# A decoder block in fp32 on one core: the first block's values summed quarter by quarter, and one written order for the first half

## The chip, the core and the metric

One core of one Trainium2 chip runs the whole program in one launch. The metric is device time in microseconds, the median of several runs of the same kernel. Beside these runs there is one profiled execution, taken by the hardware profiler; its rows are what is read below.

Six names recur. PE is the matrix engine (TensorE), PEld its weight loads, DVE is VectorE, ACT is ScalarE, POOL is GpSimd, and SP (SyncE) is the queue from which most transfers are issued. Memory on the core is SBUF; matrix products land in PSUM, which has eight banks of 128 x 512 fp32 numbers.

## The reference

A hybrid decoder block on a sequence of 2048 positions, D_MODEL 1024, eight heads of 128. Cut to what the kernel must compute:

```
c_act = silu(c)
mod = c_act @ w_mod + b_mod                    # 1024 -> 3 x 1024
shift, scale, gate = split(mod, 3)
h = rms_norm(x, g_norm) * (1 + scale) + shift  # 2048 x 1024
proj = h @ w_in                                # 2048 x 8192
x_rnn, z_rnn, q, k, v, z_attn, g_r, g_a = split(proj, 8)
xc = causal_depthwise_conv(x_rnn, conv_w, conv_b)
hr = rg_lru(xc, w_a, b_a, w_x, b_x, lam, positions)
y_rnn = (hr * silu(z_rnn)) @ w_out_rnn
o = dilated_attention_mixture(rope(q), rope(k), v)   # windows (128,1), (512,4), (2048,16)
y_attn = (o * silu(z_attn)) @ w_out_attn
merged = sigmoid(g_r + bg_r) * y_rnn + sigmoid(g_a + bg_a) * y_attn
x = x + gate * (merged @ w_o)
return rms_norm(x, g_final)
```

Nothing of `h @ w_in` can begin before a part of `mod` is known: `shift` and `scale` of the channels that the product sums over. That is why the start of the kernel consists of the modulation product.

## The kernel before

**Precision.** Every fp32 product is made of three faster products (fp32r): the high part of one operand by the high part of the other, high by low, and low by high. `mm3` issues the three through `mm` (line 151). The high part of an operand is written by ScalarE (`hi_act`, line 159), the low part, which is the operand minus its high part, by GpSimd (`lo_pool`, line 165) or VectorE (`lo_dve`, line 168). So nearly all of TensorE's instructions stand at line 151, and nearly all splits at three lines; rows are told apart by their tiles. `S` is a ring of seven tiles that hold split operands, `R` a ring of five raw tiles behind them, `T` the activations, `hf` a scratch copy. X, Z, W, V and Y are PSUM tags of pool `pj` (X has two banks, the others one), and `pg` has two banks.

**Staging.** The sequence is cut into four blocks of 512 rows, whose positions are stored so that `r` = 0..3 runs over row groups. Two halves (f = 0, 1) take two blocks each, one "even" (operands named B11 and B21, one for each half of the 1024 channels, `KH` = 4 slices `k` of 128 in each) and one "odd". For each half:

1. *Values.* `values_half` computes the v columns as plain products. Four groups `m` of 256 columns (two heads), two blocks, two halves `g` of a block's rows: 48 products of 128x128 by 128x256 for each (m, block, g), 768 in a half. `values_by_halves` does m = 0 for the even block, `values` the rest. `store_values` evicts a PSUM bank to an `ev` tile on ScalarE (line 725) and stores it to DRAM (`vN`, line 727).
2. *Strassen pairs.* The other column groups are done by pairs of 2 x 2 blocks with seven products of 12 matmuls each instead of eight. Their activation operands are B11, B21 and the combinations T1..T4 that `build_odd` makes from the odd block. Weights are loaded, split and combined ahead of their product: `operand_events` gives each step a due time in products, four products early, and `pump` runs what is due. The first half stores its split weights to DRAM, and the second reloads them.

Then attention, the output products and the final norm.

**Activations.** `load_x` loads a block; `norm_x` squares the rows on ScalarE (line 509), makes the reciprocal root, and scales each of the four row groups on VectorE (line 511). `turned` transposes four 128 x 128 tiles of slice k into one PSUM bank (line 521). `build` writes slice k: `h = scale * t + shift`, the high part on ScalarE (line 531), a full copy on ScalarE (line 534) where it must be kept, or on VectorE, and the low part on VectorE. `build_odd` does the eight slices of the odd block, and then, in eight steps, the differences (`tt`, on VectorE) and the splits of T1..T4.

**The start.** In this order in the text: load of the even block (2 x 1 MB on SP), 30 idle matmuls on constant data, parameter rows loaded and transposed (line 606), `ca = silu(c)` (lines 610 and 611), `norm_x`, four quarters of w_mod's shift and scale columns (`load_mod`, 2 x 1 MB each). Then for each quarter j: of the eight k, VectorE sums KV = 4 in rows (`acc`, lines 646 and 648), TensorE takes the other four and the `acc` rows as products with one output row (`W<-T,ca` and `W<-acc,ones`, line 151), ScalarE copies the row out (`mrow`, line 654), TensorE turns it into columns (`pg<-ones,mrow`), VectorE adds the bias and makes `mod` and `gs` (lines 666 and 667), idle matmuls follow, and the two slices k of this quarter are built. No value product of m = 0 is issued until two whole quarters (`kh` = 0) of it are built, and `w` of the values comes in halves of four k (`load_wv_half`).

**Order.** All of this is laid out by a scheduler that simulates a timeline (`schedule_with_timeline_sim`), within some orders imposed by `tc.issue_after(...)`. In stretches under `tc.manual_schedule()` the instructions go to the engines exactly as the program writes them. Before, such a stretch ran from the first half's first Strassen pair to the half's end, and another over the attention; the first half's values and the whole second half were left to the scheduler.

## Time and profile before

| | |
|---|---|
| median of three runs | 2324.31 us (2319.95, 2324.31, 2330.45) |
| profiled execution, span | 2322.0 us, 34101 instructions |
| PE busy | 2233.7 us (96%) |
| PEld busy | 1868.9 us (80%) |
| DVE busy | 1347.5 us (58%) |
| ACT busy | 1238.5 us (53%) |
| POOL busy | 971.1 us (42%) |
| transfers | 573.41 MB, 247 GB/s on the mean |
| mean granted TensorE clock | 0.984 |

The stages of the profiled execution, by TensorE's rows: the start to 49.35 us, the first half's values to 150.5, its Strassen pairs to about 750, the second half's values to 849, its Strassen pairs to 1476, attention and its products to about 2060, output to the end.

How to read the rows. A timeline row is: start, busy time, engine, line, operation, output tile <- input tiles, shape, and how many of them in a row; in brackets, how long the engine stood idle before it and what ended that. A window row gives the busy time of each engine in a stretch with the number of instructions, then the granted TensorE clock (1.00 is full), the share of the transfer engines and the rate. A group row of the page is: busy time of the group, mean ns of one | idle time of the engine just before them. A row of the waits is: engine, what waited <- what it waited for: us in all, times, mean us.

### The profile page before, as it was taken

The numbers are of one execution on the slowest core, as the hardware profiler recorded it, in microseconds if no ns is written. First come the engines' busy times: TensorE is split into PE (matmuls) and PEld (weight loads), VectorE is DVE, ScalarE is ACT, GpSimd is POOL, SyncE is SP. The second block draws the span as 40 slices with busy tenths as digits, with TensorE's granted clock in tenths as the row PEclk, the third lists the DMA queues.
The fourth block names the chain that finished last, engine by engine and source line by source line (L and its number), as shares of the span: only waits on it lengthen the run. The fifth ranks groups of instructions, "written<-read, shape, count | busy, mean of one in ns | idle before, by whom it ended". The sixth has DMA issues, their size and how long they took to land.

```text
span 2322.0 us, 34101 instructions
## 1 busy us (share of the span) xinstructions
PE 2233.7 (96%) x11459; PEld 1868.9 (80%) x11461; DVE 1347.5 (58%) x2424; ACT 1238.5 (53%) x2412; POOL 971.1 (42%) x734
## 2 busy tenths in 40 slices
PE   8999999999979998999999999999989898989998
PEld 4998788888858997877888877888879797868887
DVE  4828787768483706344444362367666777667343
ACT  4737667668433625555546311567768777534211
POOL 1457576766465333323111020446565655433100
PEclk9999999999989999999999999999999999999999
DMA  7367787887989487998776897979988888798532
GB/s 262 105 216 246 248 290 252 291 282 256 295 253 299 125 266 269 318 312 283 247 227 201 280 290 234 294 245 270 274 252 253 240 249 243 232 313 276 170 123 95
DMA packets 429013, 573.41 MB, mean 247 GB/s; under 512 B 72135, under 2 KB 293027, under 8 KB 427813
## 3 DMA queue, kind: packets, MB, share of 16 engines
q1 hardware_dynamic: 390996, 451.47, 63.3%
q10 hardware_dynamic: 37648, 119.70, 13.3%
q8 instruction: 91, 1.49, 0.3%
q14 instruction: 86, 0.70, 0.1%
q0 software_dynamic: 192, 0.05, 0.0%
HBM read 357.18 MB, written 213.91 MB: 246 GB/s over the span
## 4 chain that ended last, share of the span: by engine, by line
PE 50%; DMA 9%; DVE 4%; ACT 3%; issue 2%; POOL 1%; SPq 1%; ACTq 0%; DVEq 0%; POOLq 0%
PE pj L151 11%; PE pq L151 8%; PE X L151 7%; PE V L151 7%; PE o L151 3%; PE Y L151 3%; PE sc L151 3%; PE Z L151 3%; PE W L151 3%; DMA R<-yaT 1%; DMA vraw<-vN 1%; DMA R<-oT 1%; PE pT L1419 1%; PE pg L151 1%; DMA wD<-s 1%
## 5 line engine op out<-in xcount | busy, mean ns | idle before, releaser
L151 PE MATMUL pj<-yh,S 128*128 128x512 f32 x1024 | 369.1, 405 | 5.5 <-DMA S<-wD 4.2
L151 PE MATMUL V<-T,S 128*128 128x512 f32 x1344 | 338.7, 401 | 22.6 <-DVE t L451 9.6
L151 PE MATMUL X<-T,S 128*128 128x512 f32 x1344 | 332.5, 396 | 3.9 <-ACT u L384 3.9
L165 POOL TENSOR_TENSOR S<-R,S 128x512 fp32r<-128x512 f32 x168 | 251.9, 1510 | 181.2 <-ACT S L159 66.0
L151 PEld LDWEIGHTS V<-T,S 128*128 128x128 f32 x1344 | 257.6, 193 | 86.5 <-ACT S L159 7.9
L151 PEld LDWEIGHTS X<-T,S 128*128 128x128 f32 x1344 | 253.8, 189 | 64.4 <-ACT u L384 4.4
L151 PEld LDWEIGHTS pj<-yh,S 128*128 128x128 f32 x1024 | 194.2, 190 | 42.8 <-DVE fg L1626 4.6
L151 PE MATMUL pj<-yl,S 128*128 128x512 f32 x512 | 202.0, 395 | 0.0
L1335 ACT ACTIVATE pp<-pp,st 128x256 f32<-128x256 f32 (+3 forms) x256 | 134.0, 524 | 107.1 <-DVE st L1334 106.3
L165 POOL TENSOR_TENSOR S<-s,S 128x512 fp32r<-128x512 f32 x84 | 129.0, 1536 | 136.4 <-ACT S L159 94.6
L151 PE MATMUL W<-T,S 128*128 128x512 f32 x672 | 167.2, 397 | 0.4 <-POOL S L165 0.4
L151 PE MATMUL Z<-T,S 128*128 128x512 f32 x672 | 165.7, 395 | 0.0
L151 PE MATMUL Y<-T,S 128*128 128x512 f32 x672 | 165.4, 395 | 0.0
L151 PEld LDWEIGHTS W<-T,S 128*128 128x128 f32 x672 | 126.9, 190 | 30.8 <-issue 0.9
L151 PEld LDWEIGHTS Y<-T,S 128*128 128x128 f32 x672 | 126.7, 189 | 29.5
L151 PEld LDWEIGHTS Z<-T,S 128*128 128x128 f32 x672 | 126.3, 188 | 29.3
L168 DVE TENSOR_TENSOR ptl<-pT,pth 128x384 fp32r<-128x384 f32 (+1 forms) x160 | 97.9, 629 | 64.6 <-ACT pth L159 62.3
L159 ACT ACTIVATE S<-R 128x512 fp32r<-128x512 f32 x168 | 102.1, 622 | 48.8 <-DMA R<-in_w_in_dram 17.7
L829 DVE SCALAR_TENSOR_TENSOR xc<-xr,par,xc 128x512 f32<-128x512 f32 x96 | 93.2, 971 | 57.6 <-ACT xc L823 56.0
L1399 ACT ACTIVATE pp<-pp,M 128x256 f32<-128x256 f32 (+3 forms) x256 | 118.0, 523 | 9.0 <-DVE M L1523 9.0
L1334 DVE CUSTOM_DVE_ANT_0 pp<-sc,msk 128x256 f32<-128x256 f32 (+3 forms) x256 | 105.1, 449 | 26.0 <-PE sc L151 23.4
L165 POOL TENSOR_TENSOR vh<-vraw,vh 128x256 fp32r<-128x256 f32 (+1 forms) x64 | 67.2, 1049 | 103.5 <-ACT vh L159 91.6
(327 smaller groups left out, 4708.9 us busy)
## 6 DMA issues: line engine op xcount, KB each, us to landing
sD<-S ACTq DMA_DIRECT2D x196, 512.0 KB, 4.0
S<-sD SPq DMA_DIRECT2D x196, 512.0 KB, 5.3
S<-wD SPq DMA_DIRECT2D x99, 512.0 KB, 5.5
R<-in_w_in_dram SPq DMA_DIRECT2D x136, 256.0 KB, 4.0
wD<-s ACTq DMA_DIRECT2D x64, 256.0 KB, 5.4
T<-in_w_mod_dram SPq DMA_DIRECT2D x8, 1024.0 KB, 12.0
vN<-ev SPq DMA_DIRECT2D x64, 128.0 KB, 2.8
zaT<-ev SPq DMA_DIRECT2D x32, 256.0 KB, 3.2
```

The lines of the kernel that those rows point to most:

```text
L151: last_mm[0] = nc.tensor.matmul(o, lhsT=l, rhs=r, start=st, stop=sp, **kw).ins
L159: nc.scalar.activation(o, i, AF.Copy)
L165: nc.gpsimd.tensor_tensor(o, i, h.bitcast(F32), ALU.subtract)
L168: return nc.vector.tensor_tensor(o, i, h.bitcast(F32), ALU.subtract).ins
L829: nc.vector.scalar_tensor_tensor(xc, xr[:, i : i + CH], cw(i), xc, ALU.mult, ALU.add)
L1334: nc.vector.tensor_tensor_reduce(pdst, s_ps, mask, 1.0, 3e38, ALU.add, ALU.min, m_)
L1335: nc.scalar.activation(pdst, pdst, AF.Exp, bias=m_, scale=-1.0, accum_out=l_)
L1399: nc.scalar.activation(pp, pp, AF.Copy, scale=w)
L1419: nc.tensor.transpose(pt[:, c0 + j * P : c0 + (j + 1) * P], pp[i][:, k * P : (k + 1) * P], ident)
```

## The change

All of the first half now goes in one written order from its first load on (`manual_schedule` is entered at the top, and the `issue_after` orders are dropped). The second half's values stay with the scheduler.

* The values' weights come in quarters of two k (`raw_wv` loads, `split_wv` splits) instead of halves of four.
* The even block's values of m = 0, 1, 2 have six accumulators at once, one for each (m, g), in the six banks of `pj`. After quarter j of the modulation is known and its two slices are built, `value_sums` adds these two k to all six (24 units of 12 products in all). The products of the next quarter's modulation (`mod_products`) stand behind the third unit, its turning, bias and building (`mod_turned`, `even`) behind the fourth.
* `first_values` then does the remaining groups, (3, even), (3, odd), (0, odd), (1, odd), (2, odd), again quarter by quarter, with the loads and splits of the weights, the steps of `build_odd` and the first Strassen pairs' operand steps (`products`) put between their quarters.
* Idle matmuls: 50 at the start and 12 after `ca`, none between the quarters. The parameters' transpose and `ca` come before the norm. The first quarter has KV = 3 rows on VectorE, the others 4.
* `decay_constants` (softplus of `lam`, 26 small operations) moves behind the first quarter's six units; x1 is loaded in that quarter, squared in the third.
* `build_odd`: the low parts are deferred behind other operations, and T3's goes to GpSimd. `build` makes the kept copy of k >= 4 on VectorE instead of ScalarE. Both also hold in the second half.

```
+    order = ExitStack()
+    order.enter_context(tc.manual_schedule())
...
-    idle_matmuls(30)
+    idle_matmuls(50)
...
-    def load_wv_half(m, k):
-        wh = s_tile([P, KH, 2 * P])
-        wl = s_tile([P, KH, 2 * P])
-        for k2 in range(0, KH, 2):
...
+    def raw_wv(m, j):
+        t = raw_tile([P, 2, 2 * P])
+        rows = slice(2 * j * P, (2 * j + 2) * P)
+        nc.sync.dma_start(t[:], wcol(4 * D + m * 2 * P, 2 * P)[rows].rearrange("(k p) m -> p k m", p=P))
+        return t
+    def split_wv(t):
+        s = s_tile([P, 2, 2, 2 * P])
+        hi_act(s[:, 0], t[:])
+        lo_pool(s[:, 1], t[:], s[:, 0])
+        return s
...
         if keep is not None or first:
             hf = keep if keep is not None else T(st, [P, CH], F32, "hf", bufs=2)[:]
-            last_copy[0] = nc.scalar.activation(hf, pv, AF.Identity, bias=s, scale=g).ins
-            last_lo[0] = lo_dve(hl[:, k % KH, :], hf, hh[:, k % KH, :])
+            if keep is None or k < KH:
+                nc.scalar.activation(hf, pv, AF.Identity, bias=s, scale=g)
+            else:
+                nc.vector.tensor_scalar(hf, pv, g, s, ALU.mult, ALU.add)
+            lo_dve(hl[:, k % KH, :], hf, hh[:, k % KH, :])
...
         def split(name, k, t):
-            hh, hl = B[name]
-            hi_act(hh[:, k, :], t)
-            lo_dve(hl[:, k, :], t, hh[:, k, :])
+            hh, hl = (b[:, k, :] for b in B[name])
+            hi_act(hh, t)
+            low.append(lambda: (lo_pool if name == "T3" else lo_dve)(hl, t, hh))
...
-    for j in range(4):
-        load_mod(j)
-        if j == 1:
-            with tc.issue_after(ca_act):
-                ws0.append(load_wv_half(0, 0))
+    load_mod(0)
+    for m in range(NM):
+        load_raw(m, 0)
+    load_mod(1)
...
+    idle_matmuls(12)
+    for i in range(NM):
+        splits(i, 0)
+    load_mod(2)
+    load_mod(3)
...
+    KV = (3, 4, 4, 4)
...
-        if j < 3:
-            with tc.issue_after(last_mm[0]):
-                idle_matmuls((4, 4, 10)[j])
...
+    sums = {(m, g): T(pj, [P, 2, 256], F32, tag, bufs=1 + (tag == "X"))
+            for (m, g), tag in zip(((m, g) for m in range(NM) for g in range(2)), ("X", "X", "Z", "W", "V", "Y"))}
+    def value_sums(j, units):
+        for m, g in units:
+            for r in range(2):
+                js = slice((2 * g + r) * P, (2 * g + r + 1) * P)
+                for k in (2 * j, 2 * j + 1):
+                    (hh, hl), w = B[("B11", "B21")[k // KH]], w_v[m, j]
+                    mm3(sums[m, g][:, r, :], hh[:, k % KH, js], hl[:, k % KH, js], w[:, 0, k % 2], w[:, 1, k % 2],
+                        first=j == 0 and r == 0 and k == 0, last=j == 3 and k == KT - 1, skip_group_check=True)
...
+    def first_values():
+        odd = build_odd(vx, x1)
+        units = list(sums)
+        mod_rows(0)
+        rstd_last(ssx)
+        scale_rows(x0, ssx)
+        mod_products(0)
+        mod_turned(0)
+        even(0)
+        mod_rows(1)
+        for j in range(4):
+            for i, (m, g) in enumerate(units):
+                value_sums(j, [(m, g)])
+                if j < 3 and g:
+                    splits(m, j + 1)
+                    if (m, j) == (0, 1):
+                        x1.extend(load_x(hp, 1, "T", 14))
+                if j == 3:
+                    if i:
+                        store_values(vx, *old, sums[old[0], old[2]])
+                    old = m, 0, g
+                    if i < 4:
+                        split_raw(3, i)
+                    if i in (3, 5):
+                        next(odd)
+                if (j, i) == (2, 1):
+                    ss = squares(x1)
+                    rstd_first(ss)
+                if i == 2 and j < 3:
+                    mod_products(j + 1)
+                if i == 3 and j < 3:
+                    mod_turned(j + 1)
+                    even(j + 1)
+                    if j < 2:
+                        mod_rows(j + 2)
+                    else:
+                        rstd_last(ss)
+                        scale_rows(x1, ss)
+            if j == 0:
+                decay_constants()
...
+        for t, (m, n) in enumerate(((3, 0), (3, 1), (0, 1), (1, 1), (2, 1))):
...
+                while evicts:
+                    evicts.pop(0)()
+                for fn in steps[t, i]:
+                    fn()
+            evicts = [lambda m=m, n=n, g=g, ps=ps: store_values(vx, m, n, g, ps) for g, ps in enumerate(pss)]
...
-        values_half(f, x1)
+            values_half(f, load_x(hp, 3, "T", 14))
+        else:
+            first_values()
```

More of the change, by code (lines that the diff above doesn't have):

```diff
@@ new lines, in decoder_block @@
+    ssx = T(vx, [P, 3, 4], F32, "ssx", bufs=2)
+    for r in range(4):
+        jk = T(vx, [P, D], BF16, "hf", bufs=2)
+        nc.scalar.activation(jk[:], x0[r], AF.Square, accum_out=ssx[:, 0, r : r + 1])
+    rstd_first(ssx)
+    pt = T(pg, [P, CH], F32, "pg")
+    nc.tensor.transpose(pt[:, :N_PAR], prow[:N_PAR, :], ident[:N_PAR, :N_PAR])
+    nc.vector.tensor_copy(par[:], pt[:, :N_PAR])
+    ca = T(cp, [P, KT], F32, "ca")
+    nc.scalar.activation(ca[:], par[:, C_C : C_C + KT], AF.Sigmoid)
+    nc.vector.tensor_tensor(ca[:], ca[:], par[:, C_C : C_C + KT], ALU.mult)
@@ new lines, in decoder_block, with mod_rows @@
+    idle_matmuls(12)
[3 more added lines that the diff above has]
+    load_mod(3)
+    mod = T(cp, [P, 2, KT], F32, "mod")
+    sh = mod[:, 0, :]
+    gs = T(cp, [P, KT], F32, "gs")
+    KV = (3, 4, 4, 4)
+    acc, pr, row, pm = {}, {}, {}, {}
+    def mod_rows(j):
+        for q in range(2):
+            t = w_m[q, j]
+            acc[q] = T(vx, [P, 256], F32, "acc", bufs=4)
+            nc.vector.tensor_scalar(acc[q][:], t[:, 0, :], ca[:, 0:1], None, ALU.mult)
+            for k in range(1, KV[j]):
+                nc.vector.scalar_tensor_tensor(acc[q][:], t[:, k, :], ca[:, k : k + 1], acc[q][:], ALU.mult, ALU.add)
@@ new lines, in mod_products @@
+    def mod_products(j):
+        pr[j] = T(pg, [P, 2, 256], F32, "pg")
+        for q in range(2):
+            for k in range(KV[j], KT):
+                mm(pr[j][:1, q, :], ca[:, k : k + 1], w_m[q, j][:, k, :], q == 0 and k == KV[j], False, skip_group_check=True)
+        for q in range(2):
+            mm(pr[j][:1, q, :], ones[:, 0:1], acc[q][:], False, q == 1, skip_group_check=True)
+        row[j] = T(vx, [1, 2, 256], F32, "mrow", bufs=1)
+        nc.scalar.activation(row[j][:], pr[j][:1], AF.Copy)
```

188 lines of the change are left out of this document (105 added, 83 removed).

## The prediction

> **What bounds the kernel now.** I read the page's busy times first, then the busy time by stage, the transfers of the start, and the timeline of the first 150 us. PE rows at one line are told apart by their tiles.
>
> ```profile
> span 2322.0 us, 34101 instructions
> ...
> PE 2233.7 (96%) x11459; PEld 1868.9 (80%) x11461; DVE 1347.5 (58%) x2424; ACT 1238.5 (53%) x2412; POOL 971.1 (42%) x734
> ```
> ```profile
> core 0: us, PE busy (x) PEld busy (x) DVE busy (x) ACT busy (x) POOL busy (x), PEclk, DMA share, GB/s
> ...
> 28.30:49.35 21.05, 20.11 (x104) 9.43 (x102) 12.24 (x25) 10.36 (x16) 2.93 (x2) 1.00 0.69 236
> 49.35:100.00 50.65, 48.70 (x393) 47.91 (x393) 34.59 (x85) 37.92 (x67) 24.14 (x14) 0.97 0.41 123
> 100.00:150.49 50.49, 50.49 (x426) 50.49 (x425) 15.60 (x26) 17.33 (x30) 16.94 (x14) 1.00 0.47 142
> ```
> ```profile
> 49.35 1.34 PE L151 MATMUL V<-S,T 128*128 128x256 f32 x9
> ...
> 150.61 2.94 PE L151 MATMUL X<-T,S 128*128 128x512 f32 x12
> ```
> TensorE is busy for 96% of the span, so only its own work, or its idle time, can move the end. Its first useful value product starts at 49.35 and its first Strassen product at 150.5. Before 49.35 it looks busy (20.11 of 21.05 us), but with idle matmuls and the small modulation products. The last stretch holds nothing but value products: 50.49 / 426 = 0.1185 us each. The first half's values are 768 of them (4 quarters of the heads x 2 blocks x 2 halves x 48), 91.0 us.
>
> **The start, step by step.** In the change the first quarter of the modulation weight is enough to begin. From the timeline, and the transfers of the first 45 us (40 slices of 1.125 us):
>
> ```profile
> GB/s 0 117 174 379 433 402 434 326 350 350 349 349 346 349 350 347 347 348 349 350 350 345 356 349 345 349 350 354 340 351 346 147 23 0 0 0 0 25 346 306
> ```
> ```profile
> 1.46 8.84 PE L151 MATMUL V<-busy 128*128 128x512 bf16 x30 [1.46 <-DVE htail L763]
> ...
> 6.04 3.77 PEld L151 LDWEIGHTS <-busy 128*128 128x128 bf16 x18 [0.18 <-issue]
> ...
> 11.33 0.75 DVE L511 TENSOR_SCALAR T<-T,ss 128x1024 f32<-128x1024 f32 x1
> ...
> 15.10 0.75 DVE L511 TENSOR_SCALAR T<-T,ss 128x1024 f32<-128x1024 f32 x1
> ...
> 16.32 0.43 PE L606 MATMUL pg<-cs,prow 120*128 120x120 f32 x1
> ...
> 17.35 0.17 DVE L611 TENSOR_TENSOR ca<-ca,par 128x8 f32<-128x8 f32 x1
> ...
> 18.09 2.46 DVE L648 SCALAR_TENSOR_TENSOR acc<-T,ca,acc 128x256 f32<-128x256 f32 x6
> ...
> 36.05 1.89 PE L151 MATMUL W<-T,ca 128*1 128x256 f32 x8
> 37.77 0.59 PE L151 MATMUL W<-acc,ones 128*1 128x256 f32 x2
> 38.21 1.89 PE L151 MATMUL W<-T,ca 128*1 128x256 f32 x8
> ...
> 40.62 0.59 ACT L654 ACTIVATE mrow<-W 1x512 f32<-1x512 f32 x1 [1.66 <-PE W L151]
> ...
> 41.27 1.05 PE L151 MATMUL pg<-ones,mrow 1*128 1x1 f32 x8
> ...
> 44.41 0.60 PE L521 MATMUL pg<-cs,T 128*128 128x128 f32 x4
> ...
> 45.05 0.78 ACT L531 ACTIVATE T<-pg,mod,gs 128x512 fp32r<-128x512 f32 x1 [1.47 <-PE pg L521]
> 45.73 0.77 ACT L534 ACTIVATE hf<-pg,mod,gs 128x512 f32<-128x512 f32 x1
> ```
> Thirty idle matmuls end at 10.3, the later ones 0.21 us apart (18 in 3.77); twenty more end at 14.6. The parameter transpose then takes the place it has at 16.32, and `ca` is ready about 1 us after it, at 15.7 (1.03 from 16.32 to 17.35 before). Its twelve idle matmuls keep TensorE to 17.4. VectorE meanwhile makes six row operations of 0.41 (2.46 / 6), to 18.1, and scales x0; that took 4.5 us with its small operations (11.33 to 15.85), so 22.6. The two first w_mod pieces are the third and fourth MB in the queue: at the rates of the row they have landed by about 14.
>
> Then TensorE: one quarter's products took 1.72 + 0.44 + 1.72 + 0.44 = 4.3 us (36.05 to 40.4); the first quarter has five k instead of four, so 5.2, to 22.6. The row copy and its handover are 0.75 (to 23.4), the turning 1.05 (to 24.5), four transposes and their handover 0.85 (ACT at 25.3), then four activations 0.68 apart and the last low part 0.7: the first quarter is built at 29.0. I take **29.0** against 49.35.
>
> **What TensorE must do from there.** Moved behind the start are three quarters' products, 3 x 4.3 = 12.9 us, which were free before because TensorE was waiting; three turnings, 3.15; and all transposes but the first two. A transpose group costs 0.4:
>
> ```profile
> 82.74 1.04 PE L521 MATMUL pg<-cs,T 128*128 128x128 f32 x8
> 83.53 5.35 PE L151 MATMUL V<-S,T 128*128 128x256 f32 x43
> ```
> That is 14 x 0.42 = 5.9. With 91.0 of values the sum is 29.0 + 91.0 + 12.9 + 3.15 + 5.9 = 142.0 without any wait. Before, the same count is 49.35 + 91.0 + 1.05 + 4.2 = 145.6, and the trace has 150.5: 4.9 us of friction. So without waits the change gains 8.5, with the friction of before 3.6.
>
> The friction comes from these rows:
>
> ```profile
> 87.69 10.15 POOL L165 TENSOR_TENSOR S<-R,S 128x512 fp32r<-128x512 f32 x4 [7.20 <-PE V L151]
> ...
> 92.82 0.98 PE L151 MATMUL X<-S,T 128*128 128x256 f32 x6 [1.54 <-POOL S L165]
> 93.24 1.77 DVE L168 TENSOR_TENSOR b12l<-hx,b12h 128x512 fp32r<-128x512 f32 x1
> ...
> 94.51 5.25 PE L151 MATMUL X<-S,T 128*128 128x256 f32 x29 [0.23 <-POOL S L165]
> ...
> 99.51 0.68 DVE L168 TENSOR_TENSOR T<-hx,T 128x512 fp32r<-128x512 f32 x1
> ```
> ```profile
> 115.26 5.04 POOL L165 TENSOR_TENSOR S<-R,S 128x512 fp32r<-128x512 f32 x4 [17.42 <-PE X L151]
> ```
> ```profile
> 96.00:98.00 2.00, 2.00 (x12) 2.00 (x11) 2.00 (x2) 1.31 (x3) 1.84 (x2) 0.50 0.93 272
> ```
> A 1.54 us wait is followed by 29 products in 5.25 us where 3.4 are due, at a granted clock of 0.50: the price of a pause of that size is itself plus about 1.8.
>
> *First pause.* TensorE is nearly idle from 25.3 to 29.0, 3.7 us: I add 1.8 for a slow clock behind it (0 to 2). The Trainium skill, "TensorE: Matmul & The Clock Gate", Part 1, says the clock halves only after an idle window of about 3.4 us. By that page this pause pays the 1.8 and none of the shorter ones does, so the sum would differ little; the trace disagrees on the threshold, since 1.54 us sufficed.
>
> *Each later quarter.* After `mod_turned` the chain is: mod and gs, then the four activations and the last low part, 0.7 us behind the last of them: about 3.5 after the transposes end. It is hidden by the two units behind it (24 products, 2.84) and the first products of the next quarter (0.6). Uncovered: 0 to 1 us each, 1.0 for three (to 4, if POOL's low parts slow VectorE as at 93.24).
>
> *The end of the stage.* Alone four POOL low parts take 5.04, beside VectorE 10.15, and VectorE's own go from 0.68 to 1.77. So the two serialize. From the second of the five final steps (98 to 146) `build_odd` puts 36 two-operand operations of 0.68 on VectorE (24.5), and POOL gets 16 splits and low parts of T3 and four of the first pair at 1.26 (25.2): 50 us of work in 48. Before they had until 150 and began at 74. I add 1.4 (0 to 6) before the first Strassen products.
>
> The Trainium skill, "SBUF — State Buffer", "Who interferes with whom", gives the reason: a VectorE operation with two SBUF inputs and a GpSimd one lock each other out whole. The rows agree, and the rule speaks against moving T3's low parts to POOL; it is priced as a rival.
>
> Sum: 142.0 + 1.8 + 1.0 + 1.4 = 146.2 against 150.5, **4.3 us gained**.
>
> *New waits that I cost at nothing, and what stands behind them.*
>
> ```profile
> L699 DVE TENSOR_SCALAR e<-e 128x8 f32<-128x8 f32 x8 | 2.4, 300 | 0.0
> L698 DVE TENSOR_TENSOR e<-e,e 128x8 f32<-128x8 f32 x8 | 1.4, 171 | 0.0
> ```
> ```profile
> 71.38 0.60 ACT L725 ACTIVATE ev<-Z 128x512 f32<-128x512 f32 x1 [1.70 <-DMA vN<-ev]
> ```
> `decay_constants` now stands on VectorE between the third quarter's rows and its mod: sixteen of its 26 operations are 3.8 us, the whole under 6, and the gap is some 7. Its Exp holds ScalarE until those rows are done, with a split of w and the next row copy behind it; that split releases the R tile before the load of x1 on SyncE, and the squares of x1 then stand on ScalarE ahead of the fourth row copy. I find about 1 us of slack along this chain; each us beyond it is a us on TensorE. The six evictions come 1.42 us apart (12 products) on two `ev` tiles, so each waits for a store as at 71.38; behind them stand x1's first builds, which the first of the final steps (11.4 us of products) hides. SyncE's w_mod stream is 12.6 MB, done by 38 at the rates of the row, and TensorE asks for a quarter every 14.7 us. The dropped issue-after orders cost nothing, since the one order holds all of them.
>
> **The second half** is laid out by the scheduler again, with w in quarters, a copy moved from ScalarE to VectorE, and T3 on POOL. Waits of TensorE in 740 to 860, then in 860 to 1160:
>
> ```profile
> PE Z L151 <- POOL S L165: 1.4, 2, 1.2
> ```
> ```profile
> PE V L151 <- DVE ev L451: 3.8, 1, 3.8
> PE pg L948 <- DVE ev L943: 3.7, 1, 3.7
> PE pg L151 <- POOL xl L165: 2.9, 2, 1.4
> ```
> The value stage can give back its 1.4; I take 1.5 with some clock (-3 to +3). Of the 10.4 us behind it, the order of queues is redrawn: 0 taken, 5 either way. Everything from the first half's Strassen products to its end keeps its order and its lead, and shifts.
>
> The profiled span is 2322.0, 0.1% under the median of 2324.3; differences are carried over as they are. 2324.3 - 4.3 - 1.5 = **2318.5 us**.
>
> **Rivals.** *Smooth flow*: the frictions come out near zero and the second half loses its waits and some more: 8.5 gained in the first, 3 to 5 in the second, 2312. For it: every wait above was taken above zero, and the one order puts each quarter's chain behind two units. Against: 4.9 us of friction in the trace, which had more room. Chance 0.27.
>
> *VectorE and POOL together become the bound* (slower): T operands or first splits are late at the first Strassen products. It decides where the overrun of the 48 us passes 1.4 + 5.8 = 7.2 us. If all 36 operations cost what the one at 93.24 cost, they take 64 us, 16 over, 1.8 more for the clock: 16.4 us above my sum, 2335; half of that, 2327. For it: the rows at 87.69 to 94.51. Against: 1.77 holds a wait for a POOL operation that the 50 us count already. Chance 0.10.
>
> *It does not do what it says*: w_mod, not TensorE, paces the quarters, and the stage still ends at 149 or 150: 2323. Against: w_mod is in by 38, and the fourth quarter is asked for at 67. Chance 0.08. My forecast: 0.55.
>
> **How the numbers follow.** A measurement of this kernel tells 0.5% (11.6 us) from no change, so "within" is 2312.7 to 2335.9. The forecast and the 2323 case lie in it, except where the second half turns out 6 us better (0.07 of the 0.55). The smooth case is over the line in two thirds of its 0.27 (0.18). The slow case passes 2335.9 in a third (0.03), and a second half redrawn for the worse adds 0.05. So 0.25 faster, 0.67 within, 0.08 slower. The range takes in the smooth case with 8 us more from the second half, 2304, and most of the slow one, 2330.
>
> **What would show it.** Right: first value product at 28 to 30, quarters 14 to 15 us apart, first Strassen product at 143 to 149, the rest shifted. Wrong: value products waiting on ACT or DVE in every quarter; a wait on T or S at the first Strassen product; a clock below 1 through the stage; or a second half whose waits differ by over 5 us.

## The result, and the profile after

The changed kernel takes 2335.53 us (four runs, 2333.16 to 2342.83) beside 2322.13 of the kernel before: 1.0058 times as long, 95% interval 1.0034 to 1.0081. A second measurement gave 1.0045 (1.0027 to 1.0062). So it is 10 to 13 us slower, where 5.8 us faster was forecast, and outside the range. Ratios and intervals are those recorded with the runs; they can differ by up to 0.1% from the quotient of the two medians. Its profiled execution is the slowest of its first four runs (2342.83 us), so times are compared below stage by stage, over several profiles.

Of the page of the changed kernel, the span and the busy times:

```profile
span 2341.0 us, 34119 instructions
...
PE 2249.1 (96%) x11479; PEld 1880.1 (80%) x11479; DVE 1373.0 (59%) x2386; ACT 1234.1 (53%) x2399; POOL 984.4 (42%) x742
```
Its timeline of TensorE, at the start, at the odd block's first transposes and at the end of the first half's values:

```profile
25.31 0.80 PE L149 MATMUL X<-S,T 128*128 128x256 f32 x2 [0.43 <-ACT T L529]
26.70 1.01 PE L149 MATMUL X<-S,T 128*128 128x256 f32 x3 [0.60 <-DVE T L166]
28.04 4.32 PE L149 MATMUL X<-S,T 128*128 128x256 f32 x19 [0.33 <-DVE T L166]
...
82.08 0.30 PE L519 MATMUL pg<-cs,T 128*128 128x128 f32 x1 [0.30 <-PE W L149]
83.70 0.33 PE L519 MATMUL pg<-cs,T 128*128 128x128 f32 x1 [1.33 <-DVE T L732]
84.36 0.33 PE L519 MATMUL pg<-cs,T 128*128 128x128 f32 x1 [0.33 <-DVE T L732]
85.03 0.77 PE L519 MATMUL pg<-cs,T 128*128 128x128 f32 x5 [0.34 <-DVE T L732]
...
148.62 2.94 PE L149 MATMUL X<-T,S 128*128 128x512 f32 x12
```
The value products start at 25.3, even before the 29.0 of the prediction, since the first ones need only the first slice k. The first Strassen product comes at 148.6 against 150.6. So in these two profiles half of the gain is there, and the kernel is slower all the same.

Where it goes is read from stages. The table's times are worked out from TensorE's rows of every profile: the start of the first value product and of the first Strassen product, the length of the Strassen products 1 to 37 (to the 445th matmul record), the start of the second half's values, the length of these, of the second half's Strassen products 1 to 80, and of attention (last Strassen product to first output product). "Halves" and "quarters" is the form of the second half's value weights. The ratio to the kernel before is that of the runs.

| kernel | first value | first Strassen | 1 to 37 | second half at | its values | its 1 to 80 | attention | ratio |
|---|---|---|---|---|---|---|---|---|
| before | 49.4 | 150.6 | 110.9 | 739.1 | 110.3 | 254.3 | 621.4 | 1 |
| before_again | 48.7 | 148.3 | 110.9 | 735.3 | 110.3 | 257.2 | 622.6 | |
| second_new (quarters) | 49.4 | 150.6 | 110.9 | 736.7 | 110.8 | 260.1 | 624.1 | 1.0013 |
| after (quarters) | 25.3 | 148.6 | 116.2 | 740.7 | 113.0 | 262.3 | 627.6 | 1.0058 |
| after_again (quarters) | 26.4 | 148.9 | 115.2 | 740.4 | 110.6 | 260.3 | 626.3 | 1.0045 |
| after_scale (quarters) | 26.5 | 147.3 | 115.8 | 740.0 | 112.5 | 259.5 | 622.2 | 1.0035 |
| second_w_quarters (quarters) | 26.3 | 149.9 | 114.8 | 742.8 | 108.6 | 260.4 | 625.6 | 1.0034 |
| after_bigr (quarters) | 26.4 | 150.2 | 111.5 | 737.6 | 110.6 | 260.7 | 619.7 | 1.0037 |
| second_builds (halves) | 25.8 | 149.3 | 116.0 | 741.7 | 109.8 | 255.6 | 624.4 | 1.0019 |
| second_old (halves) | 26.0 | 148.5 | 114.6 | 739.0 | 110.3 | 256.6 | 624.6 | 1.0031 |
| second_old_again (halves) | 25.8 | 148.3 | 114.4 | 738.7 | 110.4 | 260.8 | 627.6 | 1.0023 |
| scale_early (halves) | 26.9 | 148.0 | 115.8 | 740.1 | 110.3 | 253.4 | 619.7 | 0.9998 |
| scale_early_again (halves) | 26.3 | 147.0 | 115.9 | 739.1 | 110.3 | 255.7 | 620.9 | 1.0022 |
| t3_vector (halves) | 25.2 | 147.1 | 116.7 | 737.5 | 110.3 | 258.4 | 623.5 | 1.0024 |
| fill_start (halves) | 26.9 | 149.9 | 114.6 | 740.6 | 110.3 | 253.0 | 626.3 | 1.0045 |
| low_by_act (halves) | 25.7 | 147.9 | 111.0 | 735.7 | 110.3 | 255.7 | 623.2 | 1.0008 |
| bigr_late (halves) | 25.8 | 149.1 | 111.4 | 738.0 | 110.2 | 255.0 | 622.4 | 1.0010 |
| odd_early (halves) | 25.9 | 149.4 | 111.6 | 736.6 | 110.3 | 256.4 | 625.5 | 1.0005 |
| relieved (halves) | 25.6 | 146.2 | 111.3 | 734.0 | 110.2 | 255.4 | 624.9 | 1.0013 |
| relieved_bigr (halves) | 26.8 | 146.0 | 110.9 | 733.5 | 110.7 | 256.6 | 620.8 | 1.0001 |

Two stages stand out. The first half's products 1 to 37 do so by more than they vary (110.9 before, 114.4 to 116.7 with the changed first half, until it is relieved). The second half's products 1 to 80 do so on the mean (259.5 to 262.3 in the six profiles with quarters; 253.0 to 258.4 in thirteen with halves, but once 260.8, in second_old_again). Their idle time on TensorE, the length less the busy time, is apart in every profile: 15.9 to 17.8 us with quarters, 10.5 to 15.1 with halves. Attention has one order in all of them and varies all the same:

```profile
1457.07:2084.71 627.64, 595.14 (x3626) 524.12 (x3624) 408.93 (x1109) 417.85 (x1096) 328.54 (x284) 0.98 0.84 254
```
```profile
1445.46:2065.19 619.73, 589.15 (x3626) 517.95 (x3625) 408.88 (x1109) 416.90 (x1096) 328.86 (x284) 0.99 0.84 258
```
These are the attention windows of after and of scale_early. The same 3626 instructions keep TensorE busy 6.0 us longer at the lower clock, and its weight loads 6.2; the busy times of VectorE, ScalarE and GpSimd agree within 1 us. Over the twenty profiles TensorE's idle time in attention is 29.6 to 33.7 us and the granted clock 0.973 to 0.989. A stage's single profile is no evidence there.

The first half's loss, in VectorE's rows of the changed kernel and then of the kernel before:

```profile
140.96 0.69 DVE L166 TENSOR_TENSOR T<-t,T 128x512 fp32r<-128x512 f32 x1 [0.70 <-ACT T L157]
141.57 1.79 DVE L283 TENSOR_TENSOR s<-R,R 128x512 f32<-128x512 f32 x1
143.40 1.67 DVE L284 TENSOR_TENSOR s<-s,R 128x512 f32<-128x512 f32 x1
...
161.85 0.43 DVE L913 TENSOR_SCALAR bigr<-sg 128x512 bf16<-128x512 int32 x1 [12.13 <-DMA sg<-in_positions_dram]
162.19 0.68 DVE L383 TENSOR_TENSOR u<-Z,u 128x512 f32<-128x512 f32 x1
164.82 0.43 DVE L913 TENSOR_SCALAR bigr<-sg 128x512 bf16<-128x512 int32 x1 [1.95 <-DMA sg<-in_positions_dram]
```
```profile
112.93 0.69 DVE L168 TENSOR_TENSOR T<-t,T 128x512 fp32r<-128x512 f32 x1 [0.70 <-ACT T L159]
136.36 0.69 DVE L285 TENSOR_TENSOR s<-R,R 128x512 f32<-128x512 f32 x1 [22.74 <-DMA R<-in_w_in_dram]
...
156.45 0.69 DVE L385 TENSOR_TENSOR u<-Z,u 128x512 f32<-128x512 f32 x1 [11.19 <-PE Z L151]
157.05 0.68 DVE L285 TENSOR_TENSOR s<-R,R 128x512 f32<-128x512 f32 x1
...
158.44 0.42 DVE L771 TENSOR_SCALAR bigr<-sg 128x512 bf16<-128x512 int32 x1
```
Two things have changed. The odd block's last low part is written at 141 instead of 113, so VectorE has none of its 22.7 us in hand. And the first sum of the Strassen products, `u<-Z`, waits in VectorE's queue behind `bigr<-sg`, the mask from the positions, whose load has not come: 162.2 instead of 156.5, though its product was done 2 us earlier than before. SyncE issues that load later, first of the changed kernel and then of before:

```profile
155.86 4.03 SPq L912 DMA_DIRECT2D sg<-in_positions_dram  x2
```
```profile
152.36 0.99 SPq L770 DMA_DIRECT2D sg<-in_positions_dram  x2
```
From 162 to 246 VectorE is busy for 70.1 of 84 us (66.9 before), with pauses of at most 2.9 us, and from 228 on without one. The lateness is not made up and comes out at TensorE 84 us on, where the evictions (`ev`) are missed. TensorE's row in the changed kernel, then the two rows of before:

```profile
246.36 4.60 PE L149 MATMUL V<-T,S 128*128 128x512 f32 x12 [3.49 <-DVE ev L449]
```
```profile
243.03 3.05 PE L151 MATMUL V<-T,S 128*128 128x512 f32 x12 [0.29 <-DVE ev L451]
...
255.79 3.06 PE L151 MATMUL V<-T,S 128*128 128x512 f32 x12 [1.34 <-DVE ev L451]
```
TensorE waits 3.5 us and runs its next 12 matmuls 1.6 us longer behind it (granted clock 0.63 from 246.4 to 251).

### The profile page after: what moved, and what is told of

Same layout as the page of the kernel before. It is cut to its first block, busy times and chain, and to the rows that moved or that the text cites. A ratio compares the mean times of both kernels' runs of the same rounds, so it can differ in the third digit from the quotient of the medians.

```text
span 2341.0 us, 34119 instructions
## 1 busy us (share of the span) xinstructions
PE 2249.1 (96%) x11479; PEld 1880.1 (80%) x11479; DVE 1373.0 (59%) x2386; ACT 1234.1 (53%) x2399; POOL 984.4 (42%) x742
## 3 DMA queue, kind: packets, MB, share of 16 engines
q10 hardware_dynamic: 37648, 119.70, 13.3%
## 4 chain that ended last, share of the span: by engine, by line
PE 52%; DMA 7%; DVE 5%; issue 3%; ACT 3%; POOL 1%; SPq 1%; ACTq 0%; DVEq 0%; POOLq 0%
PE pj L149 12%; PE pq L149 7%; PE X L149 6%; PE V L149 6%; PE o L149 4%; PE sc L149 4%; PE Y L149 3%; PE Z L149 3%; PE W L149 3%; PE pT L1560 1%; DMA wD<-s 1%; DMA S<-sD 1%; PE pT L1573 1%; DMA R<-yaT 1%; PE pg L149 1%
## 5 line engine op out<-in xcount | busy, mean ns | idle before, releaser
L149 PE MATMUL V<-T,S 128*128 128x512 f32 x1344 | 341.9, 404 | 26.5 <-DVE ev L449 9.4
L1475 DVE CUSTOM_DVE_ANT_0 pp<-sc,msk 128x256 f32<-128x256 f32 (+3 forms) x256 | 105.1, 449 | 29.7 <-PE sc L149 26.9
## 6 DMA issues: line engine op xcount, KB each, us to landing
R<-in_w_in_dram SPq DMA_DIRECT2D x136, 256.0 KB, 4.0
wD<-s ACTq DMA_DIRECT2D x64, 256.0 KB, 5.4
zaT<-ev SPq DMA_DIRECT2D x32, 256.0 KB, 4.1
```

The lines of the kernel that those rows point to most:

```text
L149: nc.tensor.matmul(o, lhsT=l, rhs=r, start=st, stop=sp, **kw)
L1475: nc.vector.tensor_tensor_reduce(pdst, s_ps, mask, 1.0, 3e38, ALU.add, ALU.min, m_)
```

## The experiments

Unless said otherwise each was timed in five rounds beside the kernel before; the stages are in the table.

**The halves apart.** second_old:

```
-            if keep is None or k < KH:
+            if keep is None or k < KH or half[0]:
...
-            low.append(lambda: (lo_pool if name == "T3" else lo_dve)(hl, t, hh))
+            if half[0]:
+                lo_dve(hl, t, hh)
+            else:
+                low.append(lambda: (lo_pool if name == "T3" else lo_dve)(hl, t, hh))
...
+        return [load_wv_half(m, k) for k in range(0, KT, KH)]   # in load_wv, where half[0]
```


> The first half as changed; the second half takes the form of before (values' weights in halves of four k, T3's low part at once and on VectorE, the kept copies on ScalarE). Every instruction of the second half then stands in the order of before. Theory 1, the second half: its redrawn order costs the 10 to 11 us that TensorE's rows lose between 750 and 1100, and the first half costs 1.5 (its lead of 2 at the first Strassen product is given back by VectorE before 260). Then this kernel is 1 to 4 us slower than before, 2323 to 2326. Theory 2, the first half: the loss comes from what the first half leaves behind, and the second half only shows it. Then it is 10 to 14 us slower than before, 2332 to 2336.

2330.30 us, 1.0031 (1.0018 to 1.0044). This lies between the ranges of the two theories: the first half costs more than 1.5 us, but not the whole loss.

second_w_quarters is second_old without the last of these edits, second_builds without the two others. second_old and second_w_quarters also put the mask of the second half (see below) back to its place of before, second_builds does not. That place moves nothing there: second_new, which has it as before, runs TensorE, VectorE and GpSimd through the second half in the order of the changed kernel.

> As second_old, with one of the changed kernel's edits given back to the second half: the values' weights come in quarters of two k. In the order of instructions this alone redraws the second half on all engines (148 places on TensorE, 279 on ScalarE, 104 on SyncE). Theory 1a, the quarters redraw the order: 2331 to 2336, the time of the changed kernel or within 3 us of it. Theory 1b, T3 on GpSimd and the copy on VectorE make the loss: 2323 to 2326, the time of second_old. Theory 2: the same as second_old, both at 2332 to 2336.

> As second_old, with the other two edits given back to the second half: T3's low part on GpSimd and deferred, and the kept copies of k >= 4 on VectorE. TensorE's order is the same as before. Theory 1a: no more than 2 us from second_old, 2323 to 2327, since these operations lie beside 91 us of value products. Theory 1b: 2331 to 2336, since VectorE and GpSimd lock each other out and the pair is late at the second half's first Strassen products.

1.0034 (1.0019 to 1.0048) and 1.0019 (1.0004 to 1.0033). The times do not tell them apart; the stage of products 1 to 80 does, in one profile each, first with the quarters and then with the builds:

```profile
851.34:1111.69 260.35, 243.66 (x1024) 194.78 (x1023) 121.87 (x165) 140.25 (x219) 76.44 (x61) 0.97 0.87 297
```
```profile
851.47:1107.02 255.55, 243.71 (x1025) 195.50 (x1023) 120.36 (x163) 138.44 (x219) 79.36 (x61) 0.97 0.88 299
```
TensorE is busy equally long at the same clock, and idle for 16.7 against 11.8 us.

second_new is the complement, the kernel before with the three edits in its second half alone.

> The kernel before in its first half, and the changed kernel's second half (values' weights in quarters of two k, T3's low part on GpSimd and deferred, the kept copies of k >= 4 on VectorE): every instruction of the second half in the changed kernel's order. If the second half's redrawn order costs what the profiles show (first 80 Strassen products 259.5 to 262.3 us against 253.4 to 257.2, values about 1.5 more), it is 5 to 8 us slower than before: 2327 to 2330, with the first 80 products at 259 to 262. If that stage is slow only behind the changed first half: within 2 us of before.

1.0013 (1.0003 to 1.0023), some 3 us where 5 to 8 were expected, with 260.1 in that stage: the second half's part is real without the changed first half. TensorE's two longest waits there, of second_new (us in all, times, longest):

```profile
PE pg L981 <- DVE ev L976: 6.4, 1, 6.4
PE V L151 <- DVE ev L451: 6.2, 2, 4.2
```
The prediction showed the same two of the kernel before, with 3.7 and 3.8. In the changed kernel they are 7.2 and 5.9, in second_builds 5.0 and 3.5.

**x1's scaling.** In scale_early two lines of `first_values` move ahead of the fourth quarter's `mod_products`; after_scale has the same edit in the changed kernel.

```
+                    if j == 2:
+                        rstd_last(ss)
+                        scale_rows(x1, ss)
                     mod_products(j + 1)
```


> As second_old, with one edit in the first half: the reciprocal root of x1's rows and their scaling stand on VectorE ahead of the fourth quarter's bias instead of behind its building, where VectorE stands idle for 5.4 us (66.8 to 72.2). If VectorE sets the first half's time (its last low part of the odd block stands 5 us later than before, and its chain from 160 to 256 with it): TensorE's 2.3 us of waits at 82 to 85 go, and the first half ends 2 to 3 us earlier than in second_old, 2320 to 2324. If GpSimd and VectorE's common work from 98 on sets it, which does not begin earlier: the first Strassen product comes 2 us earlier, and nothing of it is left at 260, the same time as second_old within 1 us.

> The changed kernel with the one edit of scale_early: x1's rows are scaled ahead of the fourth quarter's bias. If that edit's 6 us in the medians (2330.3 to 2324.0) is a property of the edit, the time falls by 4 to 8 us against the changed kernel measured beside it. If it was chance (the profiles show no difference of the first half at its 37th product, 263.2 and 263.8), it falls by 0 to 2.

> The kernel of scale_early, unaltered, once more. If its 6 us under second_old were the edit's: 2322 to 2325. If they were chance, as its stages say (first half 740.1 us, that of second_old 738.9): 2327 to 2330.

0.9998 (0.9988 to 1.0008), then 1.0035 (1.0020 to 1.0050; the changed kernel beside it 1.0045) and 1.0022 (1.0010 to 1.0034). The 6 us did not repeat; twelve runs of one kernel differed from eleven of the same, taken on another chip, by 0.24%, more than their intervals allow, so differences below that are not read from one measurement. The first Strassen product comes 0.5 to 1.5 us earlier and nothing of it is left at the 37th.

**The same kernels again.**

> The changed kernel, unaltered, timed in more rounds beside the kernel before. Its four times gave 0.34% to 0.81% over before. If the excess of 7 us over the two second halves that were tried one edit at a time (7.2, 7.9 and 4.4 us over before) is only chance: 2328 to 2331. If the two edits of the second half add up on top of the first half's cost: 2333 to 2337. A second profile shows how far a stage in one and the same order varies: the stage of the first half's products 1 to 37 is to repeat at 114 to 117 us (110.9 before), the second half's first 80 products at 259 to 263 (254.3 before), attention anywhere in 619 to 628.

> The kernel before, unaltered, for a second profile: how far each stage varies from one execution to the next. Products 1 to 37 of the first half at 110 to 112 us and the second half's first 80 products at 253 to 256 if these two stages are set by their order; attention within 619 to 626 if its differences between kernels are only variation.

> The kernel of second_old, unaltered, beside these. By the stages of the profiles (first half 3 us longer than before, the rest in the order of before) it should be 2 to 5 us slower than before, 2324 to 2327; its first 12 times had 2330.3. If these were right: 2329 to 2331, and then 4 us of it stand in no stage that differs in order.

1.0045 (1.0027 to 1.0062); 2321.38 us in its one run; 1.0023 (1.0012 to 1.0035). The changed kernel's time is that of its second case. The first half's stage repeats within 1 us in each kernel. The second half's products 1 to 80 do not: 257.2 after 254.3 in the kernel before, outside the 253 to 256 expected, and 260.8 after 256.6 in second_old; attention's 627.6 in second_old_again, in the order of before, makes its differences variation.

**The pair of VectorE and GpSimd.** low_by_act (one line in `split`, first half; the kernel so leaves out the low parts of T1 to T4 there and computes something else) and t3_vector (one word):

```
+                hi_act(hl, t)     # low_by_act, instead of the deferred low part
...
-                low.append(lambda: (lo_pool if name == "T3" else lo_dve)(hl, t, hh))
+                low.append(lambda: lo_dve(hl, t, hh))     # t3_vector
```


> As second_old, but in the first half the low parts of T1 to T4 are written by ScalarE as plain copies (not the low parts), so that 12 two-operand operations of VectorE and four of GpSimd are gone, some 13 us of the pair's work by their rows, for 10 us more on ScalarE, which is busy for half of that stage. If the pair VectorE and GpSimd is what takes the first half's lead back: VectorE's first operations for the Strassen pairs come 5 us earlier, products 1 to 37 take 110 to 112 us instead of 114.6, and the whole is 3 to 6 us under second_old, 2324 to 2327. If the lead is lost to something else (ScalarE's splits, the transfers): 114 to 116 us and 2328 to 2332.

> As second_old, but T3's low part stays on VectorE in the first half: four operations of 1.74 us on GpSimd become four of 0.69 on VectorE. If the two engines lock each other out, the pair gets 4.2 us less to do: products 1 to 37 take 111 to 113 us instead of 114.6, and the kernel is 1 to 4 us faster than second_old. If moving work to GpSimd relieved VectorE: 115 to 118, and 1 to 3 us slower than second_old.

low_by_act: 1.0008 (0.9993 to 1.0022), products 1 to 37 in 111.0: by its expectation the pair was the cause. t3_vector contradicts it: the pair has less to do, the first Strassen product comes 1.4 us earlier, and the 37th at the same time as in second_old (263.8 and 263.2). The two engines do slow each other: the rows at 141.57 and 143.40 take 1.79 and 1.67 beside GpSimd, that at 136.36 of before 0.69 alone. The Trainium skill, "SBUF — State Buffer", "Who interferes with whom", says that a VectorE operation with two SBUF inputs and a GpSimd operation that reads SBUF block each other; the trace agrees. But this is not the step that carries the loss.

**Earlier steps.** odd_early (these lines, and the smaller edits that its expectation names):

```
-                    if i in (3, 5):
+                    if i in (1, 3, 5):
...
-        for t, i in ((0, 0), (0, 2), (1, 0), (1, 1), (1, 3), (2, 0), (2, 1), (2, 3), (3, 0), (3, 1)):
+        for t, i in ((0, 0), (0, 1), (0, 2), (0, 3), (1, 0), (1, 1), (1, 2), (1, 3), (2, 0)):
```


> As second_old, with the pair's work of the first half begun earlier and made smaller: x1 scaled ahead of the fourth quarter's bias (as in scale_early), the odd block's builds and steps from the second unit of the fourth quarter on and one for each quarter of the following groups, T3's low parts on VectorE, the kept copies on ScalarE. The last step then stands behind the quarter that ends near 112 instead of 137. If the lateness of VectorE at 140 to 165 is what costs the first half its lead, products 1 to 37 take 110 to 112 us, the second half's first value product comes at 734 to 737 against 737.2 on the mean of the two profiles of before, and the kernel is 1 to 4 us faster than before, 2318 to 2321. If the builds now make TensorE wait in the fourth quarter or for the T operands' tiles, what is won is lost there: first Strassen product after 149, and 2322 to 2327.

1.0005 (0.9991 to 1.0019), 111.6 and 736.6, but the first Strassen product at 149.4, and so the time of its second case. TensorE waits 1.7 us for GpSimd's splits of the weights; the one at 124.25 waits 2.8 for its high part from ScalarE, which at 122.05 had waited 2.0 for an odd step on VectorE.

relieved spreads the steps, `(0, 0), (0, 1), (0, 3), (1, 0), (1, 2), (1, 3), (2, 1), (2, 2), (3, 0)`, and fills the start; fill_start has the filling alone:

```
         mod_products(0)
+        idle_sums(4)
         mod_turned(0)
         even(0)
+        idle_sums(3)
```


> As odd_early, with the odd block's steps spread a little (the last behind the quarter that ends near 126) so that GpSimd's splits of the values' weights are not held up, and with seven idle matmuls into the last accumulator's bank where TensorE waits for the first quarter's row copy and first build. If the pair and the start's slow clock are what took the gain: first Strassen product at 143 to 146, products 1 to 37 in 110 to 112.5 us, the second half's first value product at 731 to 734 (737.0 on the mean of three profiles of before's first half), and 3 to 6 us faster than before, 2317 to 2320. If the idle time only moves elsewhere: the time of odd_early, 2323 to 2326.

> As second_old, with the seven idle matmuls alone. If pauses of TensorE in the start bring the half clock (0.50 for 6.8 us from 25 to 32 in the profiles), it goes or shrinks to 3.4 us: first Strassen product 1.5 to 3.4 us earlier, 145 to 147, but the lead is lost to VectorE at product 37 (262 to 264) and the time stays that of second_old within 2 us, 2327 to 2331. If the matmuls of one output row or column themselves count as pauses, the clock stays at 0.50 from 25 to 32 and the first Strassen product at 148 to 149.

relieved: 1.0013 (1.0003 to 1.0024), first Strassen product at 146.2, 111.3, second half at 734.0: the stages as expected, the time not: 3 to 6 us faster than before were expected. fill_start: 1.0045 (1.0028 to 1.0062; five runs), with the first Strassen product at 149.9 where 145 to 147 were expected. Clock and busy times in the start, of the changed kernel and of fill_start:

```profile
24.00:28.00 4.00, 2.69 (x13) 1.85 (x11) 1.67 (x6) 3.30 (x5) 0.14 (x1) 0.66 1.10 349
28.00:32.00 4.00, 3.96 (x18) 3.96 (x19) 3.82 (x7) 0.00 (x0) 1.12 (x1) 0.50 1.10 348
```
```profile
24.00:28.00 4.00, 3.37 (x24) 2.38 (x21) 2.30 (x6) 2.05 (x4) 0.00 (x0) 1.00 1.08 345
28.00:32.00 4.00, 3.02 (x23) 2.81 (x24) 3.25 (x6) 1.34 (x3) 1.28 (x1) 1.00 1.10 349
```
The half clock is gone here and in relieved_bigr; in relieved, with the same seven matmuls, 0.59 stands in 28 to 32: they shorten it, not always to nothing. The 19 products that ran at it take 2.52 instead of 4.32 (the row at 28.04 above):

```profile
29.61 2.52 PE L149 MATMUL X<-S,T 128*128 128x256 f32 x19 [0.71 <-DVE T L166]
```
The 1.8 us are lost again at 82 to 90. TensorE comes there 1.2 us earlier than in second_old and waits 2.0 us for x1's scaling instead of 0.7, and the 24 products behind take 4.6 us instead of 3.1 (granted clock 0.66 from 85 to 90).

**The mask.** The change has one more edit, in `reset_rows`: the operations that make the mask from the loaded positions are issued with the Strassen products 2 and 3 of the half.

```
-            nc.vector.tensor_scalar(bigr[:, q * CH : (q + 1) * CH], t[:], 0, BIG, ALU.is_equal, ALU.mult)
+            later(2 + q, lambda q=q, t=t: nc.vector.tensor_scalar(
+                bigr[:, q * CH : (q + 1) * CH], t[:], 0, BIG, ALU.is_equal, ALU.mult))
```
bigr_late puts them four products later in the first half; after_bigr and relieved_bigr do the same to the changed kernel and to relieved:

```
-            later(2 + q, ...)
+            later(6 + q, ...)
```


> As second_old, with the first half's two mask operations (bigr<-sg) placed four products later, behind the first Strassen pair's sums, so that VectorE's queue no longer stands behind the load of the positions; four places of VectorE's order change and nothing else. If that wait is the step by which the lead is lost: the first sum (u<-Z) runs at 154 to 157 instead of 162.6, products 1 to 37 take 110 to 112.5 us instead of 114.5, and the kernel is 2 to 5 us faster than second_old (1.0027 times before on 23 runs), at most 1.0015. If VectorE's and GpSimd's work alone sets it: u<-Z runs earlier, but the eviction at 246 comes at the same time, 114 to 115.5 us, and 1.002 to 1.003.

> The changed kernel with this one edit in its first half. By the first theory of bigr_late: products 1 to 37 in 110 to 113 us instead of 115 to 116, the second half's first value product at 735 to 738 instead of 740.5, and 2 to 5 us faster than the changed kernel (1.0045 to 1.0058), that is 1.003 to 1.004. By the second: 1.0045 to 1.0055.

> As relieved, with this edit as well. In relieved the wait for the positions ended at 156.3, some 4 us after the first sum's product (u<-Z could run at 152). By the first theory products 1 to 37 take 109 to 110.5 us instead of 111.3 and the whole is 1 to 2 us under relieved, 0.9995 to 1.001 of before; by the second the same as relieved, 1.001 to 1.0015.

bigr_late: 1.0010 (0.9999 to 1.0021), 111.4. after_bigr: 1.0037 (1.0021 to 1.0053), 111.5, second half at 737.6. relieved_bigr: 1.0001 (0.9988 to 1.0013), 110.9, just above the 109 to 110.5 expected. VectorE's rows of bigr_late:

```profile
148.53 1.77 DVE L297 TENSOR_TENSOR s<-R,s 128x512 f32<-128x512 f32 x1 [1.18 <-POOL S L163]
154.99 0.69 DVE L383 TENSOR_TENSOR u<-Z,u 128x512 f32<-128x512 f32 x1 [4.69 <-PE Z L149]
155.59 1.53 DVE L283 TENSOR_TENSOR s<-R,R 128x512 f32<-128x512 f32 x1
...
162.94 0.43 DVE L930 TENSOR_SCALAR bigr<-sg 128x512 bf16<-128x512 int32 x1 [1.04 <-DMA sg<-in_positions_dram]
```
The last odd step is as late as in the changed kernel and the operations beside GpSimd as long; only the sum no longer stands behind the mask. It runs when its product is done, and 3.0 to 4.7 us of the stage are back (111.4 against 114.4 and 114.6; 111.5 against 116.2 and 115.2). In time, bigr_late is as its first theory has it; after_bigr's interval overlaps those of the changed kernel, so there the stage alone shows it.

All twenty profiles agree. Where the first sum starts 13.3 to 14.7 us behind the first Strassen product (eleven profiles), products 1 to 37 take 114.4 us or more; where it starts 5.8 us behind it, as before, or up to 10.4 (nine profiles), they take 110.9 to 111.6. Of the difference, 1.7 or 3.4 us are a lower granted clock (0.985 or 0.971 in the eleven, 1.000 in the nine), and the rest is waits of TensorE. So VectorE takes in 4.6 us of lateness (10.4 less 5.8) almost without loss, but not 7.5 (13.3 less 5.8), and it needs both things to lose: the mask in its new place costs little where the odd block is done early (odd_early 111.6, relieved 111.3), and a late odd block costs little where the mask stands behind (bigr_late 111.4).

With this low_by_act is to be read anew. SyncE's rows of the positions' load, of second_old and of low_by_act:

```profile
134.67 8.54 SPq L252 DMA_DIRECT2D R<-in_w_in_dram  x4
...
149.65 5.29 SPq L796 DMA_DIRECT2D vN<-ev  x4
155.01 2.49 SPq L929 DMA_DIRECT2D sg<-in_positions_dram  x2
```
```profile
147.30 2.77 SPq L794 DMA_DIRECT2D vN<-ev  x4
150.13 2.03 SPq L927 DMA_DIRECT2D sg<-in_positions_dram  x2
```
With VectorE relieved, SyncE's queue, in which raw loads wait for tiles and stores for evictions, came to the positions 4.9 us earlier. The mask runs 4.5 us earlier (157.8 against 162.2), and the first sum, still behind it, at 158.1.

## Why the prediction was wrong

*The start*: right in kind, 3.7 us too late (29.0 for 25.3), because the first slice k suffices; but the products up to 28.04 wait for their operands. *The slow clock*: 1.8 taken, 1.8 measured (4.32 against 2.52), in part by luck: it was put behind one pause of 3.7 us, and came with waits of 0.3 to 0.7. *The later quarters*: 1.0 taken; one wait of 0.7 for the third quarter's mod, which `decay_constants` delays, as the prediction said it might. *The odd block*: not in the sum; its first transposes waited 2.0 us for x1's scaling (the three rows at 83.70 to 85.03). *The end of the stage*: 1.4 taken, no wait measured at 148.62. With this the first Strassen product came at 148.6 and 148.9, not 146.2; against the mean of three profiles of the first half before (149.8) that is 1.1 us of the 4.3.

*The step that failed first*: "everything from the first half's Strassen products to its end keeps its order and its lead, and shifts." It took VectorE's order there as unchanged; one line of the change moves `bigr`, and it was not costed. It places two operations that wait for a load ahead of the first sums, on an engine that does not make up its 7.7 us (13.6 behind the first Strassen product instead of 5.8) in the next 84; and with the odd block done at 141, not 113, the load too is late. It costs 3 to 4.7 us (shown by bigr_late and after_bigr). So the second half begins at 740.5 on the mean of the six profiles with this first half (738.7 to 742.8) instead of 737.0 on that of three (735.3 to 739.1): a loss of 3.5 us where 4.3 were forecast as gained.

*The rival of VectorE and GpSimd* had the side right and the mechanism wrong: no T operand was late at the first Strassen product (148.62 has no wait), and moving T3's low parts back changed nothing at the 37th. As far as the runs show, the pair's lateness counts through the load of the mask: with the mask behind the sum (bigr_late), 111.4 of the stage remain beside 110.9.

*The second half*: "0 taken, 5 either way" and 1.5 of gain in the values. The values gained nothing, and products 1 to 80 take 260.5 on the mean of six profiles against 256.0 on that of fourteen: 4.5 us lost, at the edge of the 5 that were allowed. It comes with the weights in quarters, which move TensorE's order in the second half, where the builds leave it but for a few value products; by which of the moved instructions was not tried.

*The sum*: the first half alone costs 1.0031 and 1.0023, the second alone 1.0013; together 1.0036 to 1.0044, beside 1.0045 and 1.0058 measured. Open: the first half's 6 us in time are 2 to 3 more than its stages lose, and relieved, whose first half ends 3 us early, is not faster than before. No stage shows this part. Some of the first may be the clock: second_old's runs have a mean granted clock of 0.9828 and 0.9839, those of before beside them 0.9841 and 0.9845, and over the 139 runs of before a clock lower by 0.001 goes with 1.7 us more, which makes 1 to 2 us (an estimate). For relieved this does not hold (0.9854 beside 0.9849).

No version beats the kernel before. relieved_bigr, which has both remedies (the mask later, the odd block earlier), equals it (2320.01 beside 2321.97 us, ratio 1.0001, interval on both sides of 1).

## What to carry to other kernels

A lead is kept only if the queues behind it have slack: before an earlier start is counted as gained, look for the engine with the fewest pauses in the next stage, and for what stands in its queue ahead of the first operation that the lead needs. An operation that waits for a load, moved a few places ahead, cost 3 to 4.7 us here, more than the 1.1 by which the stage before ended earlier. And with a scheduler, an edit of tile sizes in one place can move the order of a whole half: cost it as a change of its own.

## What the runs showed of the hardware

In the changed kernel the granted clock is 0.50 from 25.4 to 32.1 us, though no wait of TensorE in the 5 us before it was over 0.7 us; these waits stand between products with one output row or column. Seven idle matmuls in two of these pauses brought 1.00 (fill_start, relieved_bigr) or a shorter slow stretch (relieved). So in these traces the clock goes by how little the array did over a stretch, and not by one long pause; whether the short waits or the narrow products count was not tried apart. The Trainium skill, "TensorE: Matmul & The Clock Gate", Part 1, has the clock halved after an idle window of about 3.4 us. No such window stands in these rows, so the measurement decides.
